# Gate and up products of ten feed-forward blocks by 1024 columns, half of their k tiles through Strassen's seven products, with pools of their own

## The chip, the cores and the metric

The kernel runs on one core of a Trainium2 chip. The metric is the device time of one execution in microseconds (us). TensorE is PE in the profile, VectorE is DVE, ScalarE is ACT; the DMA queue used is SP's.

## The reference, cut to what matters

One block of a streaming encoder on 256 tokens with a model width of 2048, in float32. Two branches and an output projection come first; the part that the change touches is the feed-forward at the end, whose hidden width is D_FF = 5632.

```python
h = h + mixed @ w_out[l]
hn = rms_norm(h, norm2_g[l])
h = h + (jax.nn.silu(hn @ w_ff_gate[l]) * (hn @ w_ff_up[l])) @ w_ff_down[l]
...
return rms_norm(h, final_g)
```

## The kernel before

Every product against a weight matrix is made of three passes. A float32 operand is split exactly into h (its upper 12 mantissa bits) and l (the rest); `mm3` adds h\*h, h\*l and l\*h in PSUM, with the activations as the stationary operand and 512 columns of weights as the moving one. The activations of the feed-forward come transposed, as tiles of 128 features by 256 tokens; two token tiles of 128 use the same weights.

Weights are read in chunks of 128 x 1024 (two k tiles by 512 columns, 512 KB). `wchunk` loads a chunk through SP's queue into `raw`, ACT makes `wh` from it (a copy that rounds) and DVE makes `wl` (a subtraction): line 67 and line 68. The pool `wp` has four buffers each of `raw`, `wh` and `wl`. `nat_group` (lines 89 to 102) takes 512 columns through all 16 k tiles: 8 chunks, 12 matmuls each, into two PSUM banks, one for each token tile.

The feed-forward goes over 11 blocks of 512 hidden columns. `ff_block` makes the gate group (line 472), SiLU on ACT with the row factor `r2`, the up group (line 476), their product on DVE, and through `transposed` (8 transposes on PE, line 150, and two splits) the operand `ah`, `al` of the down product. `down` adds the down product of several blocks into `hn`, after blocks 4, 8 and 10. The last block's down weights stay split on chip, and the final norm's pieces (`last`) come at the end.

Ahead of it, the output projection makes `h` for four times 512 columns (line 458), adds x, transposes the result into `hh`, `hl` with the norm's weight as a factor, and sums squares; `row_rstd` makes `r2` from them in a dozen small steps on DVE.

PSUM has eight banks: four `acc` and four `aux`. The order in which each engine's instructions stand is made by the framework's scheduler when the program is built; on the chip each engine then keeps its order, and waits at an instruction whose input or buffer isn't there. A tile gets a buffer when an older tile of its kind is released.

Of the kernel before, what the change touches and what calls it, by code (L numbers as in the profile page):

```python
# [8 lines left out]
F32 = mybir.dt.float32  # L9
# [24 lines left out]
WARM = 8  # matmuls of zeros that open the clock gate  # L34
# [3 lines left out]
def block_kernel(ctx: ExitStack, tc: tile.TileContext, a, out):  # L38
    """Every product against a weight matrix is float32 = three float32r passes: an operand is
    split exactly into h (its upper 12 mantissa bits, rounded) and l (the rest, 12 bits), and  # L40
    h*h + l*h + h*l is accumulated in float32."""
    nc = tc.nc
    const = ctx.enter_context(tc.tile_pool(name="const", bufs=1))
    wp = ctx.enter_context(tc.tile_pool(name="wp", bufs=4))
    tp = ctx.enter_context(tc.tile_pool(name="tp", bufs=24))
    np_ = ctx.enter_context(tc.tile_pool(name="np", bufs=11))
    sp = ctx.enter_context(tc.tile_pool(name="sp", bufs=1))
    acc_p = ctx.enter_context(tc.tile_pool(name="acc", bufs=4, space=bass.MemoryType.PSUM))
    aux_p = ctx.enter_context(tc.tile_pool(name="aux", bufs=4, space=bass.MemoryType.PSUM))

# [22 lines left out]
    def wchunk(src, cols, keep=False):  # L73
        raw = wp.tile([P, 1024], F32, tag="raw", name="raw")
        if keep:
            h, l = (t_tile(z).rearrange("p a b -> p (a b)") for z in ("kept_h", "kept_l"))
        else:
            h = wp.tile([P, 1024], F32R, tag="wh", name="wh")
            l = wp.tile([P, 1024], F32R, tag="wl", name="wl")
# [45 lines left out]
    def rsqrt(dst, src, mul, add, m, name):  # L125
        """dst = 1 / sqrt(src * mul + add), [128, m]: Newton's steps from the bits' guess, each left
        with a factor (a power of two) that the last product takes out."""
        v = sp.tile([P, m], F32, tag=f"rs_v{m}", name=f"{name}_v", bufs=2)
        y = sp.tile([P, m], F32, tag=f"rs_y{m}", name=f"{name}_y", bufs=2)
        w = sp.tile([P, m], F32, tag=f"rs_w{m}", name=f"{name}_w", bufs=2)  # L130
# [12 lines left out]
    def transposed(src, name, h, l, scale=None):  # L143
        """src [128 tokens, 2, 512] -> h, l [128, 4, 256 tokens]."""
# [14 lines left out]
    # while the first loads run: the activation table, and the tensor engine's clock  # L159
# [134 lines left out]
    # keep: 0 where a key is kept, else a large negative; [tile 1's 256 keys | tile 0's 128]  # L294
# [10 lines left out]
    # r1 * B_HEAD_DIM ** -0.5, for tile 1 and tile 0  # L305
# [147 lines left out]
    ss2 = sp.tile([P, 4, 2], F32, name="ss2")  # L453
    hn, hT = [], []
    for n in range(4):
        hx = n_tile(f"h{n}")
# [4 lines left out]
        h, l = t_tile(f"hh{n}"), t_tile(f"hl{n}")  # L461
        transposed(hx, f"h{n}", h, l, scale=g2[:, 4 * n:4 * n + 4])
        sumsq(ss2, hx, n)
        hn.append(hx)
        hT.append((h, l))
    r2 = row_rstd(ss2, "r2")

# [1 line left out]
    at = []  # L469

    def ff_block(b):
        acc = nat_group(a["w_fg"][b], KS, of(hT), f"fg{b}")
        s = n_tile(f"s{b}")
        for t in range(2):
            nc.scalar.activation(s[:, t], acc[t], AF.Silu, scale=r2[:, t:t + 1])
        acc = nat_group(a["w_fu"][b], KS, of(hT), f"fu{b}")
        for t in range(2):
            nc.vector.scalar_tensor_tensor(s[:, t], acc[t], r2[:, t:t + 1], s[:, t], op0=ALU.mult, op1=ALU.mult)
        h, l = t_tile(f"ah{b}"), t_tile(f"al{b}")
        transposed(s, f"a{b}", h, l)  # L480
        at.append((h, l))

    def down(b0, b1, n):
        acc = nat_group(a["w_fd"][n, 2 * b0:2 * b1], list(range(4 * b0, 4 * b1)), of(at), f"fd{n}")
        for t in range(2):
            nc.vector.tensor_tensor(hn[n][:, t], acc[t], hn[n][:, t], op=ALU.add)

    # the last block's weights stay split on chip, so that token tile 0 is through before tile 1
    ends = (4, 8, NFB - 1)
    b0 = done = 0  # L490
    kept = []
    for e in ends:
        for b in range(done, e + 1):
            ff_block(b)
        done = e + 1
        for n in range(4):
            down(b0, e, n)
            if e == NFB - 1:
                kept.append([wchunk(a["w_fd"][n, 2 * e + c], 1024, keep=True) for c in range(2)])
        b0 = e  # L500

    fg = []
    for i in range(2):
        f = n_tile(f"fg{i}")
# [4 lines left out]
    xh, xl = at[-1]  # L509

    def last(t, n, c0, w, ss):
        acc = acc_tile(f"last{n}")[:, :w]
        s = slice(t * P, (t + 1) * P)
        for k in range(4):
            wh, wl = (z[:, (k % 2) * 512 + c0:(k % 2) * 512 + c0 + w] for z in kept[n][k // 2])
            mm3(acc, xh[:, k, s], xl[:, k, s], wh, wl, k == 0, k == 3)
        h = hn[n][:, t, c0:c0 + w]
        nc.vector.tensor_tensor(h, acc, h, op=ALU.add)
        junk = sp.tile([P, 512], BF16, tag="junk", name="junk")
        nc.scalar.activation(junk[:, :w], h, AF.Square, accum_out=ss)  # L520

    for t in range(2):
        ss = sp.tile([P, 5], F32, tag="ss3", name="ss3", bufs=2)
        part = sp.tile([P, 1], F32, tag="part3", name="part3", bufs=2)
        r = sp.tile([P, 1], F32, tag="r3", name="r3", bufs=2)
# [7 lines left out]
        rsqrt(r, ss[:, 4:5], 1.0 / D, part, 1, "r3")  # L533
# [11 lines left out]
def _layout(np, i):  # L545
    """The arrays as the program reads them: only cut, transposed and joined."""
    x = np.asarray(i["x"])[0]

    def chunks(w, width=512, per=2):
# [3 lines left out]

    w_in = np.asarray(i["w_in"])[0]
    cuts = np.cumsum([2 * D, D, LAT, IDXH * IDXD, IDXD, IDXH])
    z, q, c, qi, ki, wi, g = np.split(w_in, cuts, axis=1)
    col = lambda v: np.asarray(v).reshape(-1, P).T  # noqa: E731
# [18 lines left out]
        "w_fg": chunks(np.asarray(i["w_ff_gate"])[0]),  # L576
        "w_fu": chunks(np.asarray(i["w_ff_up"])[0]),
        "w_fd": chunks(np.asarray(i["w_ff_down"])[0]),
# [20 lines left out]
```

## Time and profile before

| | |
|---|---|
| median of 3 runs | 1624.45 us (1624.34 to 1624.7) |
| profiled execution, span | 1624.0 us |
| TensorE busy | 1613.2 us, 99% |
| VectorE busy | 893.8 us, 55% |
| ScalarE busy | 742.9 us, 46% |
| loads and stores | 307.54 MB, 189 GB/s on the mean |

The span runs from the first to the last instruction of the profiled execution; the page gives no other time of its own for it, and the runs' median stands 0.4 us above it. Busy time is a sum over an engine's instructions; a matmul's record is longer than the distance to the next one, since matmuls are pipelined.

### The profile page before, as it was taken

The numbers are of one execution on the slowest core, as the hardware profiler recorded it, in microseconds if no ns is written. First come the engines' busy times: TensorE is split into PE (matmuls) and PEld (weight loads), VectorE is DVE, ScalarE is ACT, GpSimd is POOL, SyncE is SP. The second block draws the span as 40 slices with busy tenths as digits, with TensorE's granted clock in tenths as the row PEclk, the third lists the DMA queues.
The fourth block names the chain that finished last, engine by engine and source line by source line (L and its number), as shares of the span: only waits on it lengthen the run. The fifth ranks groups of instructions, "written<-read, shape, count | busy, mean of one in ns | idle before, by whom it ended". The sixth has DMA issues, their size and how long they took to land.

```text
span 1624.0 us, 20315 instructions
## 1 busy us (share of the span) xinstructions
PE 1613.2 (99%) x7954; PEld 1358.6 (84%) x7954; DVE 893.8 (55%) x1084; ACT 742.9 (46%) x891; POOL 1.6 (0%) x8
## 2 busy tenths in 40 slices
PE   9999999999999999999999999999999999999997
PEld 8988989889788888888888888888888888888886
DVE  5695665565754444555556444455545454554575
ACT  6554464554544444444444444444344444334452
POOL 0000000000000000000000000000000000000000
PEclk9999999999999999999999999999999999999999
DMA  8646555555545555555655555555655555555671
GB/s 302 214 138 201 187 168 182 170 177 175 163 161 192 193 193 194 193 183 196 236 186 185 194 185 190 186 191 186 194 191 192 186 191 188 193 192 194 218 253 59
DMA packets 88128, 307.54 MB, mean 189 GB/s; under 512 B 10272, under 2 KB 10528, under 8 KB 88032
## 3 DMA queue, kind: packets, MB, share of 16 engines
q1 hardware_dynamic: 88032, 306.25, 57.2%
q8 instruction: 62, 1.02, 0.2%
q14 instruction: 34, 0.28, 0.0%
HBM read 304.11 MB, written 2.10 MB: 189 GB/s over the span
## 4 chain that ended last, share of the span: by engine, by line
PE 99%; DMA 0%; DVE 0%; ACT 0%; SPq 0%; issue 0%; ACTq 0%
PE fg L85 5%; PE fg L86 5%; PE fg L87 5%; PE fu L86 5%; PE fu L87 5%; PE fu L85 5%; PE fd L87 4%; PE fd L85 4%; PE fd L86 4%; PE g L86 4%; PE g L85 4%; PE g L87 4%; PE q L120 2%; PE q L119 2%; PE q L117 2%; PE u L87 2%
## 5 line engine op out<-in xcount | busy, mean ns | idle before, releaser
L68 DVE TENSOR_TENSOR wl<-raw,wh 128x1024 fp32r<-128x1024 f32 (+1 forms) x560 | 678.9, 1212 | 668.6 <-ACT wh L67 668.2
L67 ACT ACTIVATE wh<-raw 128x1024 fp32r<-128x1024 f32 (+1 forms) x560 | 587.8, 1050 | 764.9 <-PE fu L87 139.4
L86 PE MATMUL fg<-wl,hh 128*128 128x512 f32 x352 | 137.8, 392 | 0.0
L87 PE MATMUL fg<-wh,hl 128*128 128x512 f32 x352 | 137.7, 391 | 0.0
L85 PE MATMUL fg<-wh,hh 128*128 128x512 f32 x352 | 137.1, 390 | 0.0
L85 PE MATMUL fu<-wh,hh 128*128 128x512 f32 x352 | 136.9, 389 | 0.0
L86 PE MATMUL fu<-wl,hh 128*128 128x512 f32 x352 | 136.9, 389 | 0.0
L87 PE MATMUL fu<-wh,hl 128*128 128x512 f32 x352 | 136.9, 389 | 0.0
L86 PE MATMUL fd<-wl,ah 128*128 128x512 f32 x320 | 124.8, 390 | 0.0
L87 PE MATMUL fd<-wh,al 128*128 128x512 f32 x320 | 124.8, 390 | 0.0
L85 PE MATMUL fd<-wh,ah 128*128 128x512 f32 x320 | 124.6, 389 | 0.0
L87 PE MATMUL g<-wh,xl 128*128 128x512 f32 x256 | 100.9, 394 | 0.0
L85 PE MATMUL g<-wh,xh 128*128 128x512 f32 x256 | 100.7, 393 | 0.0
L86 PE MATMUL g<-wl,xh 128*128 128x512 f32 x256 | 99.9, 390 | 0.0
L85 PEld LDWEIGHTS fu<-wh,hh 128*128 128x128 f32 x352 | 66.1, 188 | 13.7
L86 PEld LDWEIGHTS fu<-wl,hh 128*128 128x128 f32 x352 | 66.1, 188 | 13.7
L87 PEld LDWEIGHTS fu<-wh,hl 128*128 128x128 f32 x352 | 66.1, 188 | 13.7
L85 PEld LDWEIGHTS fg<-wh,hh 128*128 128x128 f32 x352 | 66.1, 188 | 13.5
L86 PEld LDWEIGHTS fg<-wl,hh 128*128 128x128 f32 x352 | 66.1, 188 | 13.4
L87 PEld LDWEIGHTS fg<-wh,hl 128*128 128x128 f32 x352 | 66.2, 188 | 13.2
L120 PE MATMUL q<-xh,wl 128*128 128x256 f32 x256 | 72.4, 283 | 0.0
L119 PE MATMUL q<-xl,wh 128*128 128x256 f32 x256 | 72.4, 283 | 0.0
(220 smaller groups left out, 2722.7 us busy)
## 6 DMA issues: line engine op xcount, KB each, us to landing
raw<-in_w_fg SPq DMA_DIRECT2D x88, 512.0 KB, 3.3
raw<-in_w_fu SPq DMA_DIRECT2D x88, 512.0 KB, 3.3
raw<-in_w_fd SPq DMA_DIRECT2D x88, 512.0 KB, 3.3
raw<-in_w_z SPq DMA_DIRECT2D x64, 512.0 KB, 3.3
raw<-in_w_g SPq DMA_DIRECT2D x64, 512.0 KB, 3.3
raw<-in_w_q SPq DMA_DIRECT2D x32, 512.0 KB, 3.3
raw<-in_w_oa SPq DMA_DIRECT2D x32, 512.0 KB, 3.3
raw<-in_w_ob SPq DMA_DIRECT2D x32, 512.0 KB, 3.3
```

Source lines behind the costliest of these rows:

```text
L67: nc.scalar.activation(h, src, AF.Copy)
L68: nc.vector.tensor_tensor(l, src, hf, op=ALU.subtract)
L85: nc.tensor.matmul(o, lh, rh, start=start, stop=False, **kw)
L86: nc.tensor.matmul(o, lh, rl, start=False, stop=False, **kw)
L87: nc.tensor.matmul(o, ll, rh, start=False, stop=stop, **kw)
L117: nc.tensor.matmul(o, wh[:, s], xh, start=(i == 0 and ct % 2 == 0), stop=False, skip_group_check=True)
L119: nc.tensor.matmul(o, wh[:, s], xl, start=False, stop=False, skip_group_check=True)
L120: nc.tensor.matmul(o, wl[:, s], xh, start=False, stop=last, skip_group_check=True)
```

## The change

Gate and up of blocks 0 to 9 are made for two blocks at a time, in groups of 1024 columns (`s_group`). For the first 8 of 16 k tiles (NS = 4 pairs) a pair of k tiles, two token tiles and two halves of the columns are taken as a 2 x 2 by 2 x 2 product, in Winograd's form of Strassen's seven products. The sums of activations are made once, in the output projection (`s_operand`). The sums of weights are made for every quad of 128 x 4 x 512 by three DVE instructions; three tiles of the weights and four of the sums are then split and multiplied. Four products go to `aux` banks (m1, m5, m7, m6) and three to `acc` banks, where the plain products of the other 8 k tiles are added. `u` and `v` combine the four; `f` adds them at the group's end. The loads are quads of 1 MB, with three buffers each of raw (which holds the sums too), `wh` and `wl`. The down product is made for two blocks at a time, one pair behind; `r2` of the up product is applied in its update of `hn`. Block 10 keeps plain products, in quads. The pools `wp`, `np` and `sp` are closed before the feed-forward, and `fp` and `wq` are opened in their place.

```diff
+NS = 4
+A12, A22, A11, S1, S3, S2, S4, A21 = range(8)
-    wp = ctx.enter_context(tc.tile_pool(name="wp", bufs=4))
-    np_ = ctx.enter_context(tc.tile_pool(name="np", bufs=11))
-    sp = ctx.enter_context(tc.tile_pool(name="sp", bufs=1))
+    pre = ExitStack()
+    wp = pre.enter_context(tc.tile_pool(name="wp", bufs=4))
+    np_ = pre.enter_context(tc.tile_pool(name="np", bufs=11))
+    sp = pre.enter_context(tc.tile_pool(name="sp", bufs=1))
...
+    def s_operand(src, name, scale):
+        raw = np_.tile([P, 8, P], F32, tag="N", name=f"{name}_raw")
+        for c, s in ((0, slice(A11, A21 + 1, A21 - A11)), (1, slice(A12, A22 + 1))):
+            nc.scalar.activation(raw[:, s], src[:, c].rearrange("p (t q) -> p t q", t=2), AF.Copy,
+                                 scale=scale[:, c:c + 1])
+        nc.vector.tensor_tensor(raw[:, S1:S3 + 1], raw[:, A22:A11 + 1],
+                                raw[:, A21:A21 + 1].to_broadcast([P, 2, P]), op=ALU.subtract)
+        nc.vector.scalar_tensor_tensor(raw[:, S2], raw[:, S1], -1.0, raw[:, A11], op0=ALU.mult, op1=ALU.subtract)
+        nc.vector.tensor_tensor(raw[:, S4], raw[:, S2], raw[:, A12], op=ALU.add)
+        h, l = (tp.tile([P, 8, P], F32R, tag="T", name=f"{name}_{z}") for z in "hl")
+        split(h, l, raw)
+        return h, l
...
-        hx = n_tile(f"h{n}")
+        hx = tp.tile([P, 2, 512], F32, tag="T", name=f"h{n}")
...
+    pre.close()
+    fp = ctx.enter_context(tc.tile_pool(name="fp", bufs=1, reuse_waits="tile"))
+    wq = ctx.enter_context(tc.tile_pool(name="wq", bufs=3, reuse_waits="tile"))
+
+    def quad(src):
+        raw = wq.tile([P, 4, 512], F32, tag="raw", name="raw")
+        nc.sync.dma_start(raw, src)
+        return raw
+
+    def quad_split(raw, n=4):
+        h = wq.tile([P, 4, 512], F32R, tag="wh", name="wh")
+        l = wq.tile([P, 4, 512], F32R, tag="wl", name="wl")
+        split(h[:, :n], l[:, :n], raw)
+        return h, l
...
+    def s_group(w, name):
+        m1, m5, m7, m6 = (aux_tile(f"{name}_{z}") for z in ("m1", "m5", "m7", "m6"))
+        c11, c12, c21, c22 = (acc_tile(f"{name}_{z}") for z in ("c11", "c12", "c21", "c22"))
+        for j in range(NS):
+            raw = quad(w[j])
+            tt = wq.tile([P, 4, 512], F32, tag="raw", name="sums")
+            nc.vector.tensor_tensor(tt[:, 0:2], raw[:, 1:3], raw[:, 0:1].to_broadcast([P, 2, 512]), op=ALU.add)
+            nc.vector.tensor_tensor(tt[:, 2], tt[:, 0], raw[:, 2], op=ALU.add)
+            nc.vector.tensor_tensor(tt[:, 3], tt[:, 2], raw[:, 3], op=ALU.add)
+            wh, wl = quad_split(raw[:, 1:4], 3)
+            th, tl = quad_split(tt)
+            xh, xl = hT[j]
+            for o, s, h, l, i in ((m1, A11, wh, wl, 0), (m5, S1, th, tl, 0), (m7, S3, th, tl, 1),
+                                  (m6, S2, th, tl, 2), (c11, A12, wh, wl, 2), (c12, S4, wh, wl, 1),
+                                  (c21, A22, th, tl, 3)):
+                mm3(o, xh[:, s], xl[:, s], h[:, i], l[:, i], j == 0, j == NS - 1 and o in (m1, m5, m6, m7))
+        u = fp.tile([P, 4, 512], F32, tag="u", name=f"{name}_u")
+        v = fp.tile([P, 2, 512], F32, tag="v", name=f"{name}_v")
+        nc.scalar.activation(u[:, 0], m1, AF.Copy)
+        nc.vector.tensor_tensor(v[:, 0], m6, u[:, 0], op=ALU.add)
+        nc.vector.tensor_tensor(u[:, 1], m7, v[:, 0], op=ALU.add)
+        nc.vector.tensor_tensor(u[:, 2], m5, v[:, 0], op=ALU.add)
+        nc.vector.tensor_tensor(u[:, 3], m5, u[:, 1], op=ALU.add)
+        for j in range(NS, KT // 2):
+            wh, wl = quad_split(quad(w[j]))
+            for c in range(2):
+                for t, i, o in ((0, 1, c11), (1, 1, c21), (0, 0, c12), (1, 0, c22)):
+                    i = (i if c == 0 else (2, 3)[i])
+                    xh, xl = h_tile(2 * j + c, t)
+                    mm3(o, xh, xl, wh[:, i], wl[:, i], o is c22 and j == NS and c == 0, j == KT // 2 - 1 and c == 1)
+        def f(t, j, dst):
+            if j == 0:
+                nc.vector.tensor_tensor(dst, (c11, c21)[t], u[:, t], op=ALU.add)
+            else:
+                nc.vector.tensor_tensor(dst, (c12, c22)[t], u[:, 2 + t], op=ALU.subtract)
+        return f
...
+    def pair_blocks(i):
+        f = s_group(a["w_fg"][i], f"fg{i}")
+        s = [f_tile(f"s{i}_{j}") for j in range(2)]
+        for j in range(2):
+            for t in range(2):
+                f(t, j, s[j][:, t])
+                nc.scalar.activation(s[j][:, t], s[j][:, t], AF.Silu, scale=r2[:, t:t + 1])
+        f = s_group(a["w_fu"][i], f"fu{i}")
+        for j in range(2):
+            up = f_tile(f"up{i}_{j}")
+            for t in range(2):
+                f(t, j, up[:, t])
+            nc.vector.tensor_tensor(s[j], s[j], up, op=ALU.mult)
+        return s
+
+    def down(b0, n_b):
+        for n in range(4):
+            acc = plain_group([a["w_fd"][n, b0 + j] for j in range(n_b)],
+                              lambda k, t: tuple(z[:, k % 4, t * P:(t + 1) * P] for z in at[b0 + k // 4]),
+                              4 * n_b, f"fd{n}")
+            for t in range(2):
+                nc.vector.scalar_tensor_tensor(hn[n][:, t], acc[t], r2[:, t:t + 1], hn[n][:, t],
+                                               op0=ALU.mult, op1=ALU.add)
+            yield n
+
+    LB = NFB - 1
+    for i in range(LB // 2):
+        s = pair_blocks(i)
+        for j in range(2):
+            a_operand(2 * i + j, s[j])
+        if i:
+            for _ in down(2 * i - 2, 2):
+                pass
```

## Rows read from the trace of the kernel before

**Rows 1.** The page: busy us, share, instructions of each engine; slices in tenths.

```profile
PE 1613.2 (99%) x7954; PEld 1358.6 (84%) x7954; DVE 893.8 (55%) x1084; ACT 742.9 (46%) x891; POOL 1.6 (0%) x8
...
PE   9999999999999999999999999999999999999997
```

**Rows 2.** The chain that ended last: shares by engine; pieces (start, us, what).

```profile
PE 99%; DMA 0%; DVE 0%; ACT 0%; SPq 0%; issue 0%; ACTq 0%
...
930.01 0.66 PE a_pt L150 x6
974.58 0.66 PE a_pt L150 x6
...
1108.30 0.66 PE a_pt L150 x6
1239.92 0.66 PE a_pt L150 x6
```

**Rows 3.** Groups of instructions by form: out<-in, shape, count | busy us, mean ns.

```profile
L68 DVE TENSOR_TENSOR wl<-raw,wh 128x1024 fp32r<-128x1024 f32 x544 | 666.5, 1225 | 659.9 <-ACT wh L67 659.5
L67 ACT ACTIVATE wh<-raw 128x1024 fp32r<-128x1024 f32 x544 | 576.6, 1060 | 757.4 <-PE fu L87 139.4 <-PE fg L87 121.6 <-PE fd L87 109.7
L86 PE MATMUL fg<-wl,hh 128*128 128x512 f32 x352 | 137.8, 392 | 0.0
...
L85 PEld LDWEIGHTS fg<-wh,hh 128*128 128x128 f32 x352 | 66.1, 188 | 13.5
...
L486 DVE TENSOR_TENSOR h<-fd,h 128x512 f32<-128x512 f32 x24 | 15.5, 683 | 4.5 <-PE fd L87 4.5
L478 DVE SCALAR_TENSOR_TENSOR s<-fu,r_r,s 128x512 f32<-128x512 f32 x22 | 15.4, 743 | 0.0
L475 ACT ACTIVATE s<-fg,r_r 128x512 f32<-128x512 f32 x22 | 15.0, 689 | 9.8 <-PE fg L87 9.8
...
L67 ACT ACTIVATE wh<-raw 128x592 fp32r<-128x592 f32 x16 | 11.1, 697 | 7.5 <-DMA raw<-in_w_kv 4.6 <-PE kv L87 1.3 <-DVE wl L68 0.9
...
L345 DVE TENSOR_TENSOR v<-v,gb 128x1024 f32<-128x1024 f32 x8 | 9.7, 1218 | 0.0
```

**Rows 4.** Waits, 886 to 1240 us: us in total, times, longest.

```profile
DVE wl L68 <- ACT wh L67: 175.1, 127, 2.3
ACT wh L67 <- PE fu L87: 75.9, 48, 1.7
ACT wh L67 <- PE fg L87: 65.8, 41, 1.7
```

**Rows 5.** DVE in order of time, end of the output projection: start, us, instruction.

```profile
883.80 1.28 DVE L460 TENSOR_TENSOR h<-out,h 128x512 f32<-128x512 f32 x2
885.38 1.23 DVE L68 TENSOR_TENSOR wl<-raw,wh 128x1024 fp32r<-128x1024 f32 x1 [0.30 <-ACT wh L67]
886.53 0.87 DVE L71 SCALAR_TENSOR_TENSOR hl<-h_pt,cols,hh 128x256 fp32r<-128x256 f32 x2
...
887.52 0.17 DVE L131 TENSOR_SCALAR r_v<-r_s 128x2 f32<-128x2 f32 x1
...
891.59 0.17 DVE L141 TENSOR_SCALAR r_r<-r_y 128x2 f32<-128x2 f32 x1
```

**Rows 6.** DMA issues by line: count, KB each, median us to landing.

```profile
raw<-in_w_fg SPq DMA_DIRECT2D x88, 512.0 KB, 3.3
```

**Rows 7.** Stretches: us, busy us of each engine (x), granted clock, DMA share, GB/s.

```profile
886.00:931.00 45.00, 45.00 (x204) 37.07 (x204) 24.97 (x36) 22.02 (x27) 0.00 (x0) 1.00 0.59 192
0.00:41.00 41.00, 39.16 (x264) 36.62 (x265) 23.84 (x38) 28.33 (x52) 1.63 (x8) 1.00 0.90 303
```

More of the change, by code (lines that the diff above doesn't have):

```diff
@@ L71, in split, with wchunk @@
             nc.vector.scalar_tensor_tensor(l, src, scale, hf, op0=ALU.mult, op1=ALU.subtract)
-    def wchunk(src, cols, keep=False):
+    def wchunk(src, cols):
         raw = wp.tile([P, 1024], F32, tag="raw", name="raw")
[L75 to L79, printed above, removed]
+        h = wp.tile([P, 1024], F32R, tag="wh", name="wh")
+        l = wp.tile([P, 1024], F32R, tag="wl", name="wl")
         nc.sync.dma_start(raw[:, :cols], src)
@@ L460, in block_kernel @@
             nc.vector.tensor_tensor(hx[:, t], acc[t], hx[:, t], op=ALU.add)
-        h, l = t_tile(f"hh{n}"), t_tile(f"hl{n}")
-        transposed(hx, f"h{n}", h, l, scale=g2[:, 4 * n:4 * n + 4])
+        if 2 * n >= NS:
+            h, l = t_tile(f"hh{n}"), t_tile(f"hl{n}")
+            transposed(hx, f"h{n}", h, l, scale=g2[:, 4 * n:4 * n + 4])
+            hT += [(z[0][:, s], z[1][:, s]) for z, s in (((h, l), slice(0, 2)), ((h, l), slice(2, 4)))]
+        else:
+            for b in range(2):
+                k = 4 * n + 2 * b
+                pt = aux_tile(f"h{n}_pt{b}").rearrange("p (c t) -> p c t", c=2)
+                for c in range(2):
+                    for t in range(2):
+                        ct = 2 * b + c
+                        nc.tensor.transpose(pt[:, c, t * P:(t + 1) * P], hx[:, t, ct * P:(ct + 1) * P], ident)
+                hT.append(s_operand(pt, f"hS{k}", g2[:, k:k + 2]))
@@ L479, in ff_block, with plain_group, a_operand @@
+    def plain_group(chunks, x, n_k, name):
+        acc = [acc_tile(f"{name}_{t}") for t in range(2)]
+        for i, c in enumerate(chunks):
+            wh, wl = quad_split(quad(c))
+            for j in range(4):
+                k = 4 * i + j
+                for t in range(2):
+                    xh, xl = x(k, t)
+                    mm3(acc[t], xh, xl, wh[:, j], wl[:, j], k == 0, k == n_k - 1)
+        return acc
+    at = {}
+    def a_operand(b, s):
         h, l = t_tile(f"ah{b}"), t_tile(f"al{b}")
@@ L480, in ff_block @@
         transposed(s, f"a{b}", h, l)
[L481 to L490, printed above, removed]
-    kept = []
[L492 to L500, printed above, removed]
+        at[b] = (h, l)
@@ new lines, in pair_blocks @@
+    def pair_blocks(i):
[8 more added lines that the diff above has]
+            up = f_tile(f"up{i}_{j}")
+            for t in range(2):
+                f(t, j, up[:, t])
+            nc.vector.tensor_tensor(s[j], s[j], up, op=ALU.mult)
+        return s
@@ new lines, in down @@
+    def down(b0, n_b):
[3 more added lines that the diff above has]
+                              4 * n_b, f"fd{n}")
+            for t in range(2):
+                nc.vector.scalar_tensor_tensor(hn[n][:, t], acc[t], r2[:, t:t + 1], hn[n][:, t],
+                                               op0=ALU.mult, op1=ALU.add)
+            yield n
@@ new lines, in block_kernel, with plain_x @@
+    LB = NFB - 1
[6 more added lines that the diff above has]
+                pass
+    def plain_x(k, t):
+        if k < 2 * NS:
+            return tuple(z[:, (A11, A12, A21, A22)[2 * t + k % 2]] for z in hT[k // 2])
+        return h_tile(k, t)
+    b = NFB - 1
+    acc = plain_group([a["w_fg10"][c] for c in range(4)], plain_x, KT, f"fg{b}")
+    s = f_tile(f"s{b}")
@@ new lines, in block_kernel @@
+    for t in range(2):
+        nc.scalar.activation(s[:, t], acc[t], AF.Silu, scale=r2[:, t:t + 1])
+    acc = plain_group([a["w_fu10"][c] for c in range(4)], plain_x, KT, f"fu{b}")
+    for t in range(2):
+        nc.vector.tensor_tensor(s[:, t], acc[t], s[:, t], op=ALU.mult)
+    a_operand(b, s)
+    kept = []
+    for n in down(b - 2, 2):
+        raw = quad(a["w_fd"][n, b])
+        kept.append([])
+        for c in range(2):
+            h, l = (tp.tile([P, 2, 512], F32R, tag="T", name=z) for z in ("kept_h", "kept_l"))
+            split(h, l, raw[:, 2 * c:2 * c + 2])
+            kept[-1].append((h, l))
@@ L552, in chunks, with strassen, quads @@
         return np.ascontiguousarray(w.transpose(3, 0, 2, 1, 4)).reshape(n // width, k // (P * per), P, per * width)
+    def strassen(w):
+        k, n = w.shape
+        w = w.reshape(k // (2 * P), 2, P, n // 1024, 2, 512).transpose(3, 0, 2, 1, 4, 5)
+        return np.stack([w[:, :, :, 0, 1], w[:, :, :, 0, 0], w[:, :, :, 1, 1], w[:, :, :, 1, 0]], axis=3)
+    def quads(w):
+        c = chunks(w, per=4)
+        return c.reshape(c.shape[:3] + (4, 512))
     w_in = np.asarray(i["w_in"])[0]
```

48 lines of the change are left out of this document (22 added, 26 removed).

## The prediction

> **What bounds the kernel now.** I read the page's engine table first, then its slices, then the chain of waits, and last the groups of instructions by form with the waits. TensorE (PE) is busy for 1613.2 of 1624.0 us and every slice of it but the last reads 9 [rows 1]; the chain that ended last is 99% PE [rows 2]. So in the feed-forward part time is the number of matmuls times their spacing. The chain gives that spacing: between the last transposes of two blocks lie 44.57 us with 192 matmuls of 512 columns and 8 transposes, and between those that have a down stage between them 131.62 us with 576 and 8 [rows 2]. The difference is 87.05 us for 384 matmuls, 0.2267 us each (the 390 ns of a matmul's own record is pipelined).
>
> VectorE (DVE) and ScalarE (ACT) have slack: a chunk of 1024 columns costs ACT 1.06 us and DVE 1.22 us [rows 3] per 12 matmuls, 2.72 us. The waits show who leads: DVE waits for ACT's split, and ACT waits for PE to free a buffer [rows 4]. The splits run as far ahead as four buffers let them, and PE never waits. The reader should see that this holds only while a stage asks DVE for less time than PE.
>
> **What the change removes.** A pair of k tiles against 1024 columns and both token tiles was 8 products of 3 matmuls; it is now 7. A group of 1024 columns falls from 192 to 4 x 21 + 4 x 24 = 180 matmuls. Ten groups (gate and up of five pairs of blocks) lose 120, or 120 x 0.2267 = 27.2 us. Block 10, the down products, the transposes and the tail keep their counts.
>
> Here a rule of the Trainium skill can be weighed. The rows give 0.2267 us for a matmul of 512 columns with its weight load. "TensorE: Matmul & The Clock Gate", section "Back-to-back issue gap", gives about 131 ns per matmul sustained at that width; by that rule the saving would be 15.7 us. The trace disagrees, over 576 matmuls in a row, and the rows are taken.
>
> **What the change adds, by stage.** A "quad" is 128 x 4 x 512 of weights, 1 MB. A DVE tensor-tensor costs 683 ns at 512 and 1225 ns at 1024 columns, 1.06 ns a column, so an estimated 1.77 us at 1536 and 2.31 us at 2048; an instruction that doesn't depend on the one before starts 0.08 us before its end (885.38 to 886.53 for a 1.23 us one) [rows 3, 5]. For ACT the rows at 592 and 1024 columns give 0.84 ns a column: 1.49 and 1.92 us. In a Strassen quad DVE does the sums, 1.22 + 0.68 + 0.68, one after the other (2.58 us), the split of three weight tiles (1.69 us net of the overlap) and of four sums (2.23 us): 6.50 us. PE needs 21 x 0.2267 = 4.76 us. ACT needs 3.4 us. In a plain quad DVE needs 2.23 us and PE 5.44 us. So DVE is 37% too slow in one half of a group and idle for most of the other. With the four sums u, v after the products and the four at the group's end (8 x 0.6), DVE has 39.7 us of work per group and PE 40.8 us: over a whole group DVE just fits. What decides is how much can be done ahead.
>
> Three buffers of each kind (raw and sums share one kind) limit that. PE still reads one through the last plain quad, so when the next group's first Strassen quad starts on PE (t = 0) at most quad 0 is split and the sums of quad 1 are made; everything else has to be made while PE runs. I follow one group by hand. The load of a quad starts when the sums two quads before are split. 512 KB lands in 3.3 us at the median, and the loads reach 303 GB/s in the first 41 us [rows 6, 7], so the second 512 KB takes 1.3 to 1.7 us more: about 4.6 us for 1 MB (bounds 3.3, as if size cost nothing, and 6.6, twice the row).
>
> Gate to up (five times). The group's last sums wait for PE, ACT then does four SiLU (690 ns each [rows 3]) before the first split: DVE ends quad 1's weights at 4.7. The buffer for the sums of quad 1 is the one that quad 0's weights free after 18 matmuls (18 x 0.2267 = 4.1); ACT then takes 1.92, to 6.1, meanwhile DVE starts quad 2's sums, then splits until 8.9. Quad 2: sums to 9.5, weights 11.2, sums' split 13.7. Quad 3, landed at 13.5: sums 16.3, weights 18.0, sums' split 20.5. PE can do the four h*h passes in the gaps and has 8 matmuls left, 22.3 us, where its own work is 84 x 0.2267 = 19.0: 3.3 us lost.
>
> Down to gate (three times). Two updates instead of SiLU: weights of quad 1 at 3.4, sums' split 8.4, quad 2 at 12.3, quad 3 lands at 13.0, its sums' split ends 19.8, PE 21.6: 2.6 us lost.
>
> Up to gate of the second pair (once): two 1024-column products and four splits of transposes (0.68 us each) lie in DVE's queue ahead of quad 1, and the transposes share the four PSUM banks with m1 to m6; part of that hides, I take 4.6 us.
>
> Entry into the first group (once). The new pools lie on the bytes of the closed ones, so loads and splits wait for the last chunks of the output projection, and the 12 small steps of r2 (887.52 to 891.59 [rows 5]), which hide now, stand in DVE's queue just then. If quad 0 is ready and quad 1 late by r2's steps, PE waits 4 us; if nothing could be made before, 11 us (a load's 4.6 and DVE's 6.5). Part of the old bytes has long been idle, so I take 7.
>
> The plain halves lose nothing: DVE does 2.23 us per 5.44 us, plus 2.4 us of sums once. The operand sums made in the output projection (four times some 2.3 us of DVE, 2.0 of ACT) lie under 96 x 0.2267 = 21.8 us of matmuls for each 512 columns; the cover is DVE's idle half there (its waits for ACT [rows 4]), and without it they would cost 9 us. The update of h becomes a scalar-tensor-tensor, 743 for 683 ns [rows 3], hidden except three times in the tail, 0.2 us. Bytes don't change, so the loads stay at 192 GB/s [rows 7].
>
> **Sum.** 5 x 3.3 + 3 x 2.6 + 4.6 + 7 = 35.9 us of PE waiting against 27.2 us saved: +8.7 us on the span of 1624.0, 1632.7; the runs' median is 0.4 us above that span, so 1633 us. Break-even is 2.7 us of waiting per group, so this is close. Bounds: with the shorter load, and quad 1's split ahead of SiLU, a group loses some 1.7, and the first entry 4 more: 1624.4 - 27.2 + 17 + 4 = 1618. With the longer load the last splits come up to 2 us later, some 5 a group. With PE's queue held in written order (the sums' products before the last two of the weights', so that a late split stops 6 matmuls that are ready, 1.4 us three times a group) it is some 7: 1624.4 - 27.2 + 70 = 1667, and 1671 with 11 at the first entry.
>
> **Rivals.** (1) DVE keeps up, and the kernel is faster. Speaks for it: DVE is busy 55% of the span [rows 1], and a group's total fits. It holds if the waiting stays under 2.4 us a group, which needs DVE to be some 2 us further ahead at t = 0 than I let it, by buffers free earlier than I think. With nothing lost in the groups and 4 us at the first entry, 1624.4 - 27.2 + 4 = 1601 us; range 1601 to 1621. Against it: 20.5 us of DVE queue after t = 0 in the count by hand above.
> (2) Queue order makes it worse: an engine's order is fixed beforehand, and a late split stops what stands behind it. For it: three engines and two kinds of buffer are now tight at once, where before only PE was [rows 4]. Above 4.9 us a group: 1646 to 1671.
> (3) The change saves less than counted, because a matmul taken away gives back only its weight load: 188 ns [rows 3], 120 x 0.188 = 22.6 us, and 1624.4 - 22.6 + 35.9 = 1638. The spacing rows speak against it. (By the rule of "TensorE: Matmul & The Clock Gate" in the Trainium skill it would be 1645.)
> (4) PE's clock falls in the waits. In the first 41 us PE was idle 1.84 us in all and the granted clock stayed 1.00, the 2.4 GHz level [rows 7]; most waits here are of that size, so I give it nothing of its own.
>
> **How the numbers follow.** Forecast case (2.4 to 4.9 us a group on the mean, 1621 to 1646): 0.55, of which 0.13 lies within 0.2% (3.2 us, about what a measurement of this kernel can tell from no change) and 0.42 above. Rival 1: 0.27, faster. Rival 2: 0.16. Rival 3: 0.02. So faster 0.27, same 0.13, slower 0.60. The range leaves out the outer part of rivals 1 and 2: 1606 to 1658.
>
> **What would show it.** Right: some 120 matmuls fewer at an unchanged 0.227 us; in a Strassen half DVE busy over 90% and PE some 85%, PE waiting for the splits of the sums; in a plain half PE full and DVE half idle; the chain no longer all PE but through DVE in ten stretches of about 19 to 23 us; one gap of 4 us or more at some 890 us. The prediction is wrong if PE stays at 99% (rival 1, then DVE was ahead at t = 0), if PE's waits lie on quads whose splits were long done (rival 2), or if loads of 1 MB land so late that DVE waits for them.

## The result, and the profile after

The changed kernel takes 1680.83 us (median of 4 runs, 1680.24 to 1683.34) against 1624.58 us in runs beside it: ratio 1.0348, 95% interval 1.0335 to 1.0361. The direction was forecast, the size was not: 56 us slower, not 9, and outside the range. The profiled execution's span is 1681.4 us, 57.4 more than before's.

The page of the changed kernel (busy us, share of the span and instructions of each engine; slices of the span in tenths, PE's busy share and PE's granted clock; shares of the chain that ended last; DMA issues with count, KB each, median us to landing) answers to [rows 1, 2, 6]:

```profile
PE 1624.3 (97%) x7834; PEld 1336.8 (80%) x7834; DVE 1105.2 (66%) x1210; ACT 783.0 (47%) x817; POOL 1.6 (0%) x8
...
PE   9999999999999999999997998999999999999997
...
PEclk9999999999999999999998999999999999999999
...
PE 81%; DVE 8%; DMA 5%; ACT 4%; issue 1%; ACTq 0%; SPq 0%; DVEq 0%
...
raw<-in_w_fg SPq DMA_DIRECT2D x44, 1024.0 KB, 4.8
```

PE has its 120 matmuls fewer (7954 to 7834) and is nevertheless busy for 11 us longer, and the chain is no longer PE alone. The slices show a dent from 883 us on, where the first Strassen group begins, with the clock in it, and one from 1009; waits of a few microseconds hardly show at 42 us a slice.

Stretches answer to [rows 7]. Columns: us, busy us of each engine with its instructions, PE's granted clock, DMA share, GB/s. First the changed kernel: one whole gate group (180 matmuls), then gate and up of block 10, which are plain (192), then four stretches of 3 us at the entry into the first group, and last two up groups, of the third and of the fifth pair:

```profile
1420.77:1467.29 46.52, 43.21 (x181) 33.34 (x180) 39.41 (x32) 22.04 (x14) 0.00 (x0) 1.00 0.49 181
...
1560.20:1604.81 44.61, 44.61 (x194) 36.17 (x192) 19.78 (x11) 16.59 (x10) 0.00 (x0) 1.00 0.59 212
...
885.00:888.00 3.00, 1.31 (x8) 0.84 (x8) 2.02 (x7) 2.60 (x8) 0.00 (x0) 0.99 0.70 240
888.00:891.00 3.00, 0.04 (x1) 0.04 (x1) 2.67 (x12) 1.93 (x3) 0.00 (x0) 0.50 1.01 426
891.00:894.00 3.00, 1.60 (x3) 0.79 (x3) 2.97 (x4) 0.00 (x0) 0.00 (x0) 0.50 0.08 33
894.00:897.00 3.00, 2.95 (x7) 2.22 (x8) 2.24 (x3) 2.37 (x2) 0.00 (x0) 0.50 0.02 5
...
1186.68:1234.77 48.09, 44.78 (x181) 34.46 (x180) 35.35 (x28) 24.07 (x17) 0.00 (x0) 0.96 0.60 219
1467.29:1513.84 46.55, 43.17 (x181) 33.41 (x180) 35.34 (x28) 24.06 (x17) 0.00 (x0) 1.00 0.63 226
```

And the kernel before, gate and up of its block 10, the same 192 matmuls:

```profile
1460.28:1503.80 43.52, 43.52 (x193) 36.05 (x192) 20.81 (x19) 18.23 (x18) 0.00 (x0) 1.00 0.59 193
```

Three things are to be seen. Block 10, which the change leaves alone but for its buffers, takes 44.61 us for 43.52 with PE full in both: 0.2323 us a matmul instead of 0.2267. A Strassen group takes 46.52 us where 180 matmuls at that spacing take 41.82: 4.7 us of waiting, none of it at the clock's expense. At the entry PE stands nearly still for 5 us, and its granted clock falls to 0.50, the 1.2 GHz level, for some 10 us. Two shorter falls, of 3.4 us, lie at 922 and 1208 us. The group with the second one, an up group, takes 48.09 us where its like takes 46.55; the two keep step within 0.05 us until the fall, so this fall costs some 1.5 us. The waits ahead of it (1.6, 1.9 and 1.0 us) stand in the other group as well, where the clock stays at 1.00.

The account, stage by stage (a stage is counted from its first matmul in the timeline to the next stage's; waits are its length less its matmuls at 0.2323 us and its transposes):

| term | forecast, us | measured, us |
|---|---|---|
| 120 matmuls fewer | -27.2 | -27.2 |
| spacing of the 2952 matmuls that read the new weight buffers, 5.7 ns each | 0 | +16.8 |
| entry into the first group | +7 | +20.9 |
| up to gate, second pair | +4.6 | +7.6 |
| gate to up, five times | +16.5 | +26.9 |
| down to gate, three times | +7.8 | +14.2 |
| sum | +8.7 | +59.2 |

The span grew by 57.4; the 1.8 us left over are mostly transposes (sixteen in a row take 1.77 us, twice eight took 2.10, five times). The entry is counted from the start of the run: 0.6 of its 20.9 us lie ahead of the output projection, whose start differs by up to 3 us between runs with the same spacing up to there.

### The profile page after: what moved, and what is told of

Its sections match the earlier page's. It is cut to its first block, busy times and chain, and to the rows that moved or that the text cites. A ratio compares the mean times of both kernels' runs of the same rounds, so it can differ in the third digit from the quotient of the medians.

```text
span 1681.4 us, 19677 instructions
## 1 busy us (share of the span) xinstructions
PE 1624.3 (97%) x7834; PEld 1336.8 (80%) x7834; DVE 1105.2 (66%) x1210; ACT 783.0 (47%) x817; POOL 1.6 (0%) x8
## 4 chain that ended last, share of the span: by engine, by line
PE 81%; DVE 8%; DMA 5%; ACT 4%; issue 1%; ACTq 0%; SPq 0%; DVEq 0%
DVE wl L74 5%; PE fd L90 4%; PE fd L89 4%; PE fd L88 4%; ACT wh L73 4%; PE g L89 3%; PE g L90 3%; PE g L88 3%; DMA raw<-in_w_fu 3%; DMA raw<-in_w_fg 2%; PE fu_c L88 2%; PE fu_c L90 2%; PE fu_c L89 2%; PE q L120 2%; PE q L123 2%; PE q L122 2%
## 5 line engine op out<-in xcount | busy, mean ns | idle before, releaser
L74 DVE TENSOR_TENSOR wl<-raw,wh 128x1024 fp32r<-128x1024 f32 (+3 forms) x432 | 636.8, 1474 | 434.5 <-ACT wh L73 433.8
L73 ACT ACTIVATE wh<-raw 128x1024 fp32r<-128x1024 f32 (+3 forms) x432 | 544.3, 1260 | 643.1 <-PE fd L90 100.6
L74 DVE TENSOR_TENSOR wl<-sums,wh 128x2048 fp32r<-128x2048 f32 x40 | 91.6, 2290 | 38.9 <-ACT wh L73 38.7
L73 ACT ACTIVATE wh<-sums 128x2048 fp32r<-128x2048 f32 x40 | 76.6, 1914 | 73.5 <-PE fg_c L90 30.2
L120 PE MATMUL q<-xh,wh 128*128 128x256 f32 x256 | 72.4, 283 | 0.0
L89 PEld LDWEIGHTS fd<-wl,ah 128*128 128x128 f32 x320 | 60.3, 188 | 13.9
L90 PEld LDWEIGHTS fd<-wh,al 128*128 128x128 f32 x320 | 60.2, 188 | 13.9
L88 PE MATMUL fu_c<-wh,hh 128*128 128x512 f32 x160 | 62.8, 403 | 3.0 <-ACT wh L73 3.0
L90 PE MATMUL fu_c<-wh,hl 128*128 128x512 f32 x160 | 63.2, 395 | 0.0
L90 PE MATMUL fg_c<-wh,hl 128*128 128x512 f32 x160 | 63.2, 395 | 0.0
L89 PE MATMUL fu_c<-wl,hh 128*128 128x512 f32 x160 | 63.1, 395 | 0.0
L89 PE MATMUL fg_c<-wl,hh 128*128 128x512 f32 x160 | 63.1, 394 | 0.0
```

Of the source, the lines that this page charges most:

```text
L88: nc.tensor.matmul(o, lh, rh, start=start, stop=False, **kw)
L89: nc.tensor.matmul(o, lh, rl, start=False, stop=False, **kw)
L90: nc.tensor.matmul(o, ll, rh, start=False, stop=stop, **kw)
L120: nc.tensor.matmul(o, wh[:, s], xh, start=(i == 0 and ct % 2 == 0), stop=False, skip_group_check=True)
```

## The experiments

Waits of a group below are its length less its matmuls at that run's own spacing; the entry is counted as in the table. A run with one time is compared with a run of the kernel before beside it (1624.6 each time); the changed kernel's own four runs lie 3.1 us apart, so less than that between two single runs says nothing.

**The place of the weights' buffers** (e1_place). The pools' sizes put the upper and lower parts (wh, wl) of before, and the stationary tiles of both kernels, at 1952 bytes mod 2048; the new pools put wh and wl at 1312.

```diff
     wq = ctx.enter_context(tc.tile_pool(name="wq", bufs=3, reuse_waits="tile"))
+    gap = fp.tile([P, 160], F32, name="gap")
+    nc.gpsimd.memset(gap[:, :1], 0.0)
```

> 640 bytes are laid ahead of the weight buffers of the changed kernel, so that they start at the same offset in 2048 bytes as the weight buffers of the kernel before; nothing else changes. Theory (the place of the moving operand sets the spacing of the matmuls): 0.2267 us again in place of 0.2324 us over 2952 matmuls that read these buffers, 16.8 us less, some 1664 us. Rival (the spacing comes from higher addresses, the larger tiles, or the traffic of DVE, ACT and the loads): 0.232 us and some 1681 us.

1675.58 us. Stretch of block 10, and a gate group, in this run:

```profile
1554.60:1598.12 43.52, 43.52 (x193) 36.04 (x192) 19.77 (x11) 16.59 (x10) 0.00 (x0) 1.00 0.61 218
1414.78:1460.92 46.14, 42.58 (x181) 33.26 (x180) 38.57 (x31) 21.56 (x13) 0.00 (x0) 1.00 0.50 182
```

640 bytes give the old spacing back, to the hundredth of a microsecond. Only 5 us of the 16.8 reach the end (7.8 between the two profiled executions). The groups now wait 5.3 us and more (46.14 less 180 at 0.2267): PE comes sooner to splits that are no earlier. And behind the first group the granted clock falls in four groups here, in one of the changed kernel; the three up groups among the four take 1.3 to 2.2 us more than one without a fall (46.17 us). The plain stages keep the gain, the Strassen groups hand most of it to the wait and to the clock.

**Places again, both operands** (e11_same_place). The tiles of x and of the activations are moved to 1312 as well; wh and wl of the stages before, by the same move, lie at 288.

```diff
+    shift = const.tile([P, 96], F32, name="shift")
...
     tp = ctx.enter_context(tc.tile_pool(name="tp", bufs=24))
+    cw = ctx.enter_context(tc.tile_pool(name="cw", bufs=1))
...
-    warm = const.tile([P, 512], BF16, name="warm")
+    warm = cw.tile([P, 512], BF16, name="warm")
...
+    gap = fp.tile([P, 416], F32, name="gap")
```

> Only places: the tiles of x and of the activations (the stationary operands) start at 1312 mod 2048 like the weights' upper and lower parts of the feed-forward blocks, which stay at 1312; the weights' buffers of the stages before lie at 288, unlike their stationary tiles (one of the six F tiles is given up for the room). Theory: the spacing depends on where the moving operand lies against the stationary one, so the feed-forward stages, alike again, go back to 226.7 to 227 ns, while the stages before (288 against 1312) rise to 231 ns or more. Rival: 1312 is a bad place by itself: 232.4 ns in the feed-forward stages, and in the last stage too, whose kept tiles lie at 1312 now (227.5 ns there so far). Of the time only the sum of the two is expected: 1665 to 1690 us.

1674.19 us. Block 10 in this run, and below it in the run e6_entry further down, where wh and wl lie at 1600 against 1952:

```profile
1553.12:1596.64 43.52, 43.52 (x194) 36.05 (x192) 19.77 (x11) 16.60 (x10) 0.00 (x0) 1.00 0.62 218
```

```profile
1578.05:1623.03 44.98, 44.98 (x193) 36.16 (x192) 19.80 (x11) 16.59 (x10) 0.00 (x0) 1.00 0.60 210
```

So 1312 is no bad place by itself (the rival falls): beside stationary tiles at 1312 it gives 226.7 ns, beside 1952 it gave 232.3. The half of the theory that the stages before would slow down was wrong: with wh and wl 1024 bytes off (288 against 1312) they keep 226.9 ns on the mean. The second token tile's operand starts 512 bytes behind the first's, so a stage has one difference only mod 512. Moving less stationary, mod 512: 0 gives 226.7 to 226.9 (before, e1_place, e11_same_place in both parts), 384 gives 232.3, 160 gives 234.3 (e6_entry), 352 gives 231 to 237 by the pass (e6_entry, stages before). What counts is how the two operands of a matmul lie to each other; the rule within 512 bytes stays open, since these are the only differences that ran.

**One part alone: pools and loads without the seven products** (e9_plain). NS = 0: all quads plain, so the same matmuls as in the kernel before.

```diff
-NS = 4
+NS = 0
...
-        for j in range(NS):
-            raw = quad(w[j])
...
+            nc.scalar.activation(dst, (c11, c21, c12, c22)[2 * j + t], AF.Copy)
```

> One part alone: NS = 0, that is the new pools, 1024 KB loads and four accumulators of the change, with all eight quads of each gate and up group plain (24 matmuls each) and no sums, no Strassen operands. Theory: what the new pools cost by themselves is the spacing, about 3070 matmuls of these stages by 5.7 ns = 17.5 us, and an entry of 8 to 16 us: 1648 to 1658 us, so that the seven products themselves (27.2 us of matmuls saved, 10 groups with 5 us of waits and more) make the rest of the way to 1681, a loss of 23 to 33 us. Rival: the 232.4 ns belong to the seven products' tiles of x (128x8x128 instead of 128x4x256), and the pools cost only the entry: 1632 to 1641 us with 226.7 ns.

1652.55 us, +28.0: 17.4 of it spacing (3072 matmuls), 9.2 the entry, and no waits in any later group. The first gate group, and block 10 again, 44.62 us:

```profile
891.51:938.90 47.39, 47.02 (x192) 37.59 (x193) 22.82 (x11) 18.93 (x11) 0.00 (x0) 0.95 0.60 209
...
1529.51:1574.13 44.62, 44.62 (x193) 36.18 (x192) 19.80 (x11) 16.59 (x10) 0.00 (x0) 1.00 0.60 213
```

The pools, with the larger loads and groups, cost half of the loss, and the seven products the other half, 28.3 us on top: 27.2 saved and some 55 waited. They gain nothing in this form.

**The entry: where the pools lie** (e2_pools, e6_entry). In the changed kernel the first load goes out at 884.75, when the last out chunk's buffers are free. e2_pools opens the pools that close in the order np, sp, wp, so that the first quads lie on bytes free earlier (and a gap of 1056 bytes keeps the stages before at 1952); e6_entry also puts the small scratch of the norms into a pool of its own.

```diff
-    wp = pre.enter_context(tc.tile_pool(name="wp", bufs=4))
     np_ = pre.enter_context(tc.tile_pool(name="np", bufs=11))
     sp = pre.enter_context(tc.tile_pool(name="sp", bufs=1))
+    gap = sp.tile([P, 264], F32, name="gap")   # e2_pools alone
...
+    wp = pre.enter_context(tc.tile_pool(name="wp", bufs=4))
...
+    late = ctx.enter_context(tc.tile_pool(name="late", bufs=1))   # e6_entry: junk, ss2, s2, rs_*
```

> The pool of the old weight buffers is opened after the two others, so that the new raw buffers lie on bytes that have long been idle (a gap keeps the old weight buffers at their offset). Theory (PE waits at the first group because the first load may not start before the last chunks of the output projection are done, and the clock falls in that wait): the load starts before 870 us, the first group waits 4 to 6 us in place of 21.6, no stretch at 1.2 GHz there: 1664 to 1667 us. Rival (DVE's queue with r2's small steps makes the wait): 4 us less at most, 1677 us.

> Only places are changed: the small scratch of the norms (junk, ss2, r2's and r3's temporaries) goes into a pool of its own that is never closed, and the three pools that close are opened in the order np, sp, wp, so that the first group's raw quads, sums and upper parts lie on bytes that have been idle for long. Theory: the 21.6 us that TensorE waits around the entry of the first group (5.2 at the end of the out stage, 16.4 in the first gate group, the half clock in it included) come from buffers that wait for the norm's chain and the last out chunks; with that wait gone the first load goes out in the out stage, sums and splits run under it, and about 5 of the 16.4 us are left (the wait of any Strassen group), no half clock near 890: 1666 to 1672 us. Rival: the engines' queues hold the entry up (the first group's splits stand behind the norm's chain on VectorE and ScalarE wherever the buffers lie): 1676 to 1682 us. The buffers' places move too (wh and wl start at 1600 mod 2048 instead of 1312): the spacing of the matmuls that read them, 232.4 ns after and 226.9 in the run with the places of before, shows by itself whether 1600 belongs to the one or the other.

e2_pools took 1685.45 us, e6_entry 1701.79 (of the latter some 10 us are the spacing of the stages before, which its places spoil, and some 6 that of the groups). Both theories fell; that the engines' queues hold the entry up is what is left. The timeline of SyncE's and of DVE's instructions in e6_entry (start, us, instruction, idle time before it and its releaser):

```profile
875.84 0.86 SPq L506 DMA_DIRECT2D raw<-in_w_fg  x2
```

```profile
886.24 1.22 DVE L75 TENSOR_TENSOR wl<-raw,wh 128x1024 fp32r<-128x1024 f32 x1 [1.58 <-ACT wh L74]
895.65 1.40 DVE L478 TENSOR_TENSOR h<-out,h 128x512 f32<-128x512 f32 x2 [8.19 <-PE out L91]
897.93 0.16 DVE L218 TENSOR_REDUCE r_s<-ss 128x2 f32<-128x8 f32 x1 [0.89 <-ACT junk L214]
...
901.53 1.22 DVE L528 TENSOR_TENSOR sums<-raw 128x1024 f32<-128x1024 f32 x1
```

The load went out 20 us before PE's last out product, and DVE then idles for 8.19 us: the first sums stand in its queue behind the update of h, which waits for that product, and behind r2's steps. They start at 901.53 although their quad landed at 882.55. So an earlier load alone gains nothing. In the changed kernel the quad lands at 889.40, and the sums start at 890.38, right behind r2, with the same wait for PE (7.88 us) ahead of them: the two waits end within 1 us of each other. No run changed DVE's order at the entry.

**Half as many Strassen quads** (e5_two_pairs), `NS = 2`, everything else as in the change.

> Strassen's products for 2 pairs of k tiles of 8 in place of 4; the rest plain. Gives back 60 matmuls, 13.6 us. Theory (what is ready ahead covers the first quad and the sums of the second, so the waits lie in the last two quads of four): the wait falls from 5.0 to about 0.7 us a group, 1681 + 13.6 - 43 = some 1652 us. Rival (each Strassen quad costs its share): 2.5 us a group, 1670 us.

1650.0 us, as the first theory has it. A gate group:

```profile
1392.05:1436.16 44.11, 43.73 (x188) 34.88 (x186) 31.41 (x24) 19.04 (x12) 0.00 (x0) 1.00 0.53 192
```

It waits 0.9 us (44.11 us less 186 matmuls at 0.2323), and the entry 13.5. The wait is no toll of a Strassen quad; it comes when four follow each other.

**Order of the splits** (e3_sums_first). th, tl are split before wh, wl.

```diff
-            wh, wl = quad_split(raw[:, 1:4], 3)
             th, tl = quad_split(tt)
+            wh, wl = quad_split(raw[:, 1:4], 3)
```

> In a Strassen quad the sums are split before the weights (two lines swapped). Theory (in each group's last quad the weights' split stands in DVE's queue ahead of the third sum, so ACT gets the sums late and DVE idles 2.65 us): some 2.4 us less in each of ten groups, about 1657 us. Rival (three buffers and DVE's total are what limits): under 5 us less, 1676 us or more.

1714.17 us: 33 us more than the change, where 24 less were expected. DVE in the timeline of a group:

```profile
1460.74 0.69 DVE L529 TENSOR_TENSOR sums<-sums,raw 128x512 f32<-128x512 f32 x1
1463.49 2.29 DVE L74 TENSOR_TENSOR wl<-sums,wh 128x2048 fp32r<-128x2048 f32 x1 [2.06 <-ACT wh L73]
```

With nothing between the last sum and the split of the sums, DVE waits some 2 us for ACT's copy in every Strassen quad, and a later group waits 6.9 to 9.9 us and more, a fall of the granted clock included, which each of the ten groups has here. The split of the weights was the cover for that copy.

**A longer ring** (e7_raw4). Raw quads and sums get four buffers, paid for with two F tiles.

```diff
-        return fp.tile([P, 2, 512], F32, tag="F", name=name, bufs=6)
+        return fp.tile([P, 2, 512], F32, tag="F", name=name, bufs=4)
...
-        raw = wq.tile([P, 4, 512], F32, tag="raw", name="raw")
+        raw = wq.tile([P, 4, 512], F32, tag="raw", name="raw", bufs=4)
...
-            tt = wq.tile([P, 4, 512], F32, tag="raw", name="sums")
+            tt = wq.tile([P, 4, 512], F32, tag="raw", name="sums", bufs=4)
```

> One part: the ring that holds raw quads and their sums has 4 buffers instead of 3 (the F tiles give up two of their six to make room). Theory: the 5.0 us that each Strassen group waits in its last quad come from the ring: the load of that quad goes out only when the sums of the quad before last are split, and a fourth buffer lets it go out some 5 us sooner, so that half or more of the wait goes: 2 to 2.5 us in each of the ten groups, 1650 to 1660 us. Rival: VectorE's own work sets it (6.62 us of sums and splits a Strassen quad against 4.76 us of matmuls, four quads in a row), and an earlier load gains at most the 1.0 us that VectorE waits for it: 4 to 5 us a group, 1668 to 1681 us.

1657.1 us, 24 less than the change. A gate group:

```profile
1397.94:1442.73 44.79, 42.60 (x181) 33.57 (x180) 38.38 (x32) 21.93 (x14) 0.00 (x0) 1.00 0.52 188
```

It waits 3.0 us instead of 4.7, and the entry 13.9 instead of 20.9. The ring is part of the cause, and not all: two thirds of a group's wait stay.

**Strassen and plain quads by turns** (e10_interleave), with u and v behind the last quad.

```diff
+        for j in range(NS):
+            strassen(j)
+            plain(NS + j)
```

> One order: each gate and up group takes its quads as Strassen, plain, Strassen, plain and so on, instead of four Strassen quads and then four plain ones; the combinations u and v stand behind the last quad. Theory: the 5 us of each group are VectorE's work on four Strassen quads in a row (6.62 us against 4.76 of matmuls each), which the ring of three buffers can't carry; a Strassen quad with a plain one behind it asks 8.9 us of VectorE against 10.2 of matmuls, so the wait falls to 0.5 to 1.5 us a group: 1636 to 1646 us, the entry staying at 16 to 22 us. Rival: the wait is the chain load, sums, copy, split of each Strassen quad (about 14 us from issue to its last split), which one plain quad doesn't cover either: 4 us or more a group, 1670 us or more; or the u and v chain, now between the last matmul of a group and the next group's first product, takes the place (3 to 5 us a group: 1660 to 1675).

1663.76 us. A gate group behind a down stage, then the up group behind it:

```profile
1404.56:1446.63 42.07, 42.07 (x181) 33.65 (x180) 34.02 (x29) 20.85 (x14) 0.00 (x0) 1.00 0.49 175
1446.63:1494.36 47.73, 44.64 (x181) 34.14 (x180) 39.36 (x32) 25.34 (x17) 0.00 (x0) 0.96 0.57 205
```

Both were right in part: the gate group waits 0.25 us, with four Strassen quads as before, so alternating cures the run of four; the up group waits 5.9, since its first sums share DVE with the gate group's eight combinations (these and the first of the sums fill DVE from 1441.12 to 1447.5 in the timeline; the sums' split ends at 1454.7). Its clock fell too (0.96), and yet it is no longer than the up group before it, 47.73 us at 1.00: this fall lay where PE waited anyway.

**The causes mended together** (c4_order, c3_order, c2_order): a plain quad first, Strassen quads apart, u and v under a plain quad, four raw buffers (and four F tiles for six), weights at 1952; with four, three and two Strassen quads a group. The first product into an accumulator is now a plain quad's. The core of the one with three:

```diff
-NS = 4
+NS = 3
...
+        todo = [list(range(NS)), list(range(NS, KT // 2))]
+        for z in "PSPSPSPP":
+            (strassen, plain)["SP".index(z)](todo["SP".index(z)].pop(0))
```

> Three of the causes mended together, four Strassen quads kept (P plain, S Strassen): the order P S P S P S S P, so that no group begins with sums and u and v lie under a plain quad; a fourth raw buffer; weights at 1952 mod 2048. Theory (spacing 16.8 us, waits of 5 us a group by VectorE's work in a row and the ring of three, entry 21.6 us by the first group's four Strassen quads): 226.8 ns, 1 to 2 us of waits a group, entry 8 to 12: 1612 to 1630 us. Rival: VectorE has 41 us of work (8 splits, 4 sums, 8 combinations) for 40.8 us of matmuls in a group of four, so that some 3 us a group stay whatever the order: 1632 to 1645 us.

> The same with three Strassen quads a group, order P S P S P S P P (20.4 us of matmuls saved instead of 27.2, VectorE's work 36.7 us a group for 41.5 us of matmuls). Theory: under 1 us of waits a group, entry 8 to 10: 1612 to 1624 us. Rival (waits of each Strassen group stay above 2 us by the combinations between two groups): 1626 to 1640 us.

> The same with two Strassen quads a group, order P S P P S P P P (13.6 us of matmuls saved). Theory: about 0.5 us of waits a group, entry 8: 1618 to 1625 us, that is at or just below the kernel before. Rival (combinations): 1628 us or more.

| kernel | median us | ratio to before, 95% interval |
|---|---|---|
| c4_order | 1654.85 | 1.0184 (1.0169 to 1.0199) |
| c3_order | 1612.3 | 0.9923 (0.9906 to 0.9939) |
| c2_order | 1619.08 | 0.9963 (0.995 to 0.9976) |

The page of c3_order, its chain, and two stretches: gate and up group of the third pair, and 3 us at the entry:

```profile
PE 1594.7 (99%) x7864; PEld 1342.9 (83%) x7864; DVE 1061.0 (66%) x1170; ACT 767.6 (48%) x807; POOL 1.7 (0%) x9
...
PE 98%; DMA 0%; DVE 0%; ACT 0%; issue 0%; ACTq 0%
```

```profile
1106.39:1189.35 82.96, 82.96 (x368) 68.69 (x366) 67.53 (x52) 42.93 (x28) 0.00 (x0) 1.00 0.60 216
...
888.00:891.00 3.00, 1.27 (x3) 1.08 (x4) 1.93 (x5) 2.28 (x2) 0.00 (x0) 0.50 1.01 426
```

366 matmuls in 82.96 us are 0.2267 each: no wait and the old spacing, with DVE busy 81% of the stretch. c3_order is faster than both kernels, 0.8% faster than the one before; what is left of the loss is an entry of 7.6 us, with the clock still at half in part of it. c4_order waits mostly where a group follows another one; there PE waits at the first Strassen quad and at the two adjacent ones:

```profile
1263.45:1304.80 41.35, 41.33 (x182) 33.59 (x180) 32.99 (x26) 21.33 (x13) 0.00 (x0) 1.00 0.53 182
1304.80:1352.26 47.46, 43.47 (x181) 32.79 (x180) 39.64 (x34) 24.36 (x18) 0.00 (x0) 1.00 0.54 204
```

The gate group waits 0.55 us, the up group 6.7 (8.1 in others, where the clock fell). That goes beyond its rival's 3 us a group, and it doesn't lie in every group, as the rival has it: the total of DVE's work is not what is short (it is busy for 33.0 and 39.6 us in the two groups, for 40.8 us of matmuls each), but what it can make ahead of a group that follows another one. The order, the ring and the places were not taken apart again at NS = 3.

## Why the prediction was wrong

The sum missed by 50.5 us: 16.8 by the spacing, 13.9 by the entry, 3.0 by up to gate, 16.8 by the other groups (10.4 gate to up, 6.4 down to gate).

**Right:** 120 matmuls less; 1 MB in 4.8 us (4.6 forecast, though its lower step of 1.3 us follows from no row: 512 KB at 303 GB/s are 1.7); DVE's sizes (2.29 and 1.75 us for 2.31 and 1.77); PE's 86% in a Strassen half; the chain through DVE; a gap at some 890 us; waits in every group, in the last Strassen quad.

**Two signs that did not come.** The two halves of the gate group shown above:

```profile
1420.77:1445.02 24.25, 20.94 (x86) 15.45 (x85) 19.57 (x15) 14.13 (x9) 0.00 (x0) 1.00 0.50 176
1445.02:1467.29 22.27, 22.27 (x97) 17.89 (x96) 19.84 (x18) 7.91 (x6) 0.00 (x0) 1.00 0.49 187
```

In the Strassen half DVE is busy for 81%, not over 90%, and in the plain half for 89%, not half: it works ahead there, and then stands idle for 4.7 us in the half where PE waits for it. "DVE is 37% too slow" is not all of it; what DVE waits for counts as well.

**Wrong, "an unchanged 0.227 us".** 16.8 us of the miss. The sum carried the spacing of before [rows 2] over to buffers in another place, and "the plain halves lose nothing" with it: they don't wait, and yet every plain stage lost 2.5%. In the text it looked like a property of the matmul; e1_place and e11_same_place show that it is one of the two operands' places. The Trainium skill ("TensorE: Matmul & The Clock Gate", section "Step-by-step: what each phase is for") says that the streamed operand and the weight load have a read port each, so that loading the next tile takes nothing from the running matmul. The places matter here all the same, 226.7 against 232.3 ns for the same instructions. Whether it is the weight load that the streamed operand meets, no run here shows.

**Mis-sized, the waits of a group** (3.3 and 2.6 us forecast, 5.4 and 4.7 measured on the mean). The count by hand took DVE's instructions of a quad in the order three sums, weights, sums' split, with ACT's copy of the sums hidden under the weights. DVE and ACT of the changed kernel in the last Strassen quad of the group that starts at 1140.12:

```profile
1153.70 1.23 DVE L527 TENSOR_TENSOR sums<-raw 128x1024 f32<-128x1024 f32 x1 [1.04 <-DMA raw<-in_w_fg]
1154.96 0.69 DVE L528 TENSOR_TENSOR sums<-sums,raw 128x512 f32<-128x512 f32 x1
1155.57 1.75 DVE L74 TENSOR_TENSOR wl<-raw,wh 128x1536 fp32r<-128x1536 f32 x1
1157.24 0.69 DVE L529 TENSOR_TENSOR sums<-sums,raw 128x512 f32<-128x512 f32 x1
1160.57 2.29 DVE L74 TENSOR_TENSOR wl<-sums,wh 128x2048 fp32r<-128x2048 f32 x1 [2.65 <-ACT wh L73]
```

```profile
1158.14 0.60 ACT L541 ACTIVATE fg_u<-fg_m 128x512 f32<-128x512 f32 x1 [2.94 <-PE fg_m L90]
1158.64 1.90 ACT L73 ACTIVATE wh<-sums 128x2048 fp32r<-128x2048 f32 x1
```

The quad landed 13.5 us after the group's start, near the 13.0 counted, and DVE waited 1.04 us for it, which the prediction had named as a sign of being wrong. The last sum then comes behind the weights' split, and ACT's copy of the sums stands behind the copy of m1, which waits for PE; DVE idles 2.65 us, and its last split ends at 22.7 us, not 19.8. Rival 2 named the cause (an order fixed beforehand stops what stands behind it), at 4.9 us a group or more, and its chance was too small; its sign, waits of PE on quads whose splits were long done, did not come: PE waited for the last quad's own splits. What the order costs was not priced by itself: e3_sums_first changed it for the worse, e7_raw4 took 1.7 us of 4.7 by the ring, and e10_interleave and c3_order took the wait away where they spread the quads.

Up to gate (4.6 forecast, 7.6 measured) was taken without working. It fell to 4.0 us with the longer ring (e7_raw4) and to 0.1 in c3_order.

**Mis-sized, the entry** (7 forecast with 11 as the bound, 20.9 measured). "Part of the old bytes has long been idle" looked at the buffers. e6_entry shows that the first sums stand in DVE's queue behind the last product of the stage before, so nothing is made ahead, though their quad had landed. The rest grows with the Strassen quads of the first group: 9.2 us with none (e9_plain), 13.5 with two (e5_two_pairs), 20.9 with four, and 7.6 with three that stand apart (c3_order, with the longer ring and the old places too).

**Wrong, rival 4.** It was given nothing on waits of 1.84 us in all over 41 us [rows 7]. The waits here came closer together and longer, and between 880 us and the last stage the granted clock fell to 0.50 three times. The short fall at 1208 us cost 1.5 us; the long one and the one at 922 us lie in the 20.9 us of the entry and were not priced by themselves.

The terms are not independent: e1_place gave 16.8 us of spacing back and kept 5, since a faster PE waits more for the same DVE and its clock fell in three groups more.

## What to carry to other kernels

An algorithm like this one takes matmuls away and moves work to the engine that prepares operands: compare the two engines per buffer ring, not per stage, and spread the costly quads among cheap ones before giving up. Look at the order in which each engine will take its instructions; data that lands early gains nothing behind a queued instruction that waits. When pools move, compare the spacing of a stage that was not changed before anything else.

## What the runs showed of the hardware

A matmul of 512 float32r columns came every 226.7 to 226.9 ns when its two operands' buffers started 0 mod 512 bytes apart, every 232.3 ns at 384, every 234.3 ns at 160, and every 231 to 237 ns, by the pass, at 352. VectorE kept its queue's order: in e6_entry it stood idle for 8.19 us with a landed quad behind an instruction that waited for PE. The granted clock halved at waits of PE of 1 to 4.4 us in a 97% busy kernel and was back 3.4 us (twice) and 10.2 us (once) later; the same waits in another group of the same run left it at 1.00. One fall of 3.4 us cost 1.5 us, and one that lay under a wait (e10_interleave) nothing.
